# Attention scores as two products of 128 rows and one of 32 rows in two row groups

## The chip, the cores and the metric

The kernel runs on one core of a Trainium2 chip. The metric is the device time of one execution in microseconds (us), the median over runs. Before the change it is 2363.67 us (three runs, 2359.02 to 2363.83).

Engines are named as in the profile: PE is TensorE's matmul, PEld its weight load, DVE is VectorE, ACT ScalarE, POOL GpSimd, and SP is the engine that issues most DMAs. A product on PE has a stationary operand (up to 128 rows by 128 columns, loaded by a LDWEIGHTS on PEld) and a moving operand (the same rows by up to 512 columns). The sum runs over the rows, which are the partitions of on-chip memory where both operands lie. A product whose operands have 32 rows uses one of four 32-row groups of the array.

## The reference, cut to what matters

Two layers, each with latent attention beside a convolution module, and then a gated feed-forward part. What the change touches is the attention's scores: 8 heads, 1024 tokens, 64 "nope" components and 32 rotary ("rope") components a head. The rotary part of the key is one for all heads.

```python
sc = (jnp.einsum("bqhd,bkhd->bhqk", qn, k_nope)
      + jnp.einsum("bqhr,bkr->bhqk", qr, k_rope))
p = jax.nn.softmax(sc.astype(jnp.float32) * scale, axis=-1).astype(v.dtype)
return jnp.einsum("bhqk,bkhd->bqhd", p, v)
```

All is float32. The kernel gets near that accuracy by splitting each operand into a high and a low part, rounded to the one-pass type float32r, and adding three products: high by high, high by low and low by high.

## The kernel before, in words

A layer is three stages. `project` makes the latents, queries, keys and the convolution's input; `attention` makes values, scores, softmax and the weighted sum; `feed` does the output projection and the feed-forward part. PE, DVE, ACT and POOL run in the order in which the program writes them (`manual_schedule`); the DMAs on SP's queue are ordered by a planner, by when their inputs are ready.

Keys and queries are split into high and low parts in `project` and written to scratch in device memory: `kd` (keys, nope), `krd` (key, rope), `qd` (queries, nope) and `qrd` (queries, rope, in two halves of 16 rows). Head 0 (`DIRECT = 1`) doesn't go through scratch: the steps `key`, `query_rope` and `query` also copy its parts from on-chip memory straight into its operand tiles on SP's queue (L566, L567, L592, L607). Every other head is brought in by `load_head` (L249), called in the loop of `attention` when the head before it is at its third block (L1405). A head has four operand tiles (`head_tiles`, L1246): q high, q low, k high, k low, each of 96 rows (64 nope, 32 rope), from a pool with 8 slots ("m"). So a head's tiles come free when the scores of the head two before it are done. Most other large tiles come from a pool of 31 slots ("b", through `blk`).

The attention loop runs over blocks n = head x 8 + query tile, 64 a layer, 128 in all. For one n the order on PE is:

- `turn(n)`: eight transposes (tile t) of the softmax numerators, which ACT copies and DVE subtracts to high and low parts;
- `scores(n + 2)`: six products of 96 rows by 512 columns into a two-bank tile s: for each column half, (high, high), (high, low), (low, high); then DVE takes the negated row maximum mx;
- `expo(n + 1)` on ACT: the exponential of an earlier s;
- `values(...)`: eight products of 128 rows by 256 columns into the tile o.

Beside it, an `agenda` puts other work at given n: the convolution's late taps (`tap_late`, L1438: a product on POOL or ACT, then an addition on POOL or by an accumulating DMA), and from n = 56 on the weights of the output projection (tile wo): POOL issues a DMA of the high half, ACT turns it to its negative (L166, at n = 59), POOL adds the input by DMA (L167).

At the start of a layer's attention PE makes the first value tiles (`rows`, L1271, tile pv) and then the scores of block 0; these need head 0's tiles whole.

Of the kernel before, what the change touches and what calls it, by code (L numbers as in the profile page):

```python
# [10 lines left out]
F32R = mybir.dt.float32r  # L11
# [9 lines left out]
NOPE = 64  # L21
ROPE = 32
HALF = ROPE // 2
# [48 lines left out]
HALVES = (slice(0, 512), slice(512, T))  # L72
# [33 lines left out]
class Encoder:  # L106
# [301 lines left out]
    def project(self, l, carry):  # L408
        nc, a = self.nc, self.a
# [4 lines left out]
        heads = {}  # L414
        qd = [self.dp.tile([HEADS, NOPE, T], F32R, name=f"qd{l}{i}") for i in range(2)]
        qrd = [self.dp.tile([2, HEADS, HALF, T], F32R, name=f"qrd{l}{i}") for i in range(2)]
        kd = [self.dp.tile([HEADS, NOPE, T], F32R, name=f"kd{l}{i}") for i in range(2)]
        krd = [self.dp.tile([ROPE, T], F32R, name=f"krd{l}{i}") for i in range(2)]
        st = {}
# [65 lines left out]
        def latent(name, out, key, j):  # L485
            c = self.blk(f"c{name}{l}")
            nc.vector.tensor_tensor(out=c, in0=ps[name], in1=rx, op=ALU.mult)
            out.append(c)
            if j == 0:
                st[key] = self.blk(f"{key}{l}")  # L490
                nc.scalar.activation(out=st[key], in_=c, func=AF.Square)
                yield 1.22, 0.0
                return
            sq = self.blk(f"{key}{l}_{j}")
            nc.scalar.activation(out=sq, in_=c, func=AF.Square)
            yield 1.22, 1.5
            nc.vector.tensor_tensor(out=st[key], in0=st[key], in1=sq, op=ALU.add)
            yield 1.25, 0.0
# [56 lines left out]
        def key(j):  # L555
            if j == 0:
                heads.update((h, self.head_tiles(l, h)) for h in range(DIRECT))
            p = ps[f"k{j}"]
            kh, kl = self.blk(f"kh{l}_{j}", F32R), self.blk(f"kl{l}_{j}", F32R)
            nc.scalar.copy(out=kh, in_=p)  # L560
            yield 0.0, 1.5
            nc.vector.tensor_tensor(out=kl, in0=p, in1=kh.bitcast(F32), op=ALU.subtract)
            for i, s in enumerate((kh, kl)):
                self.move(kd[i][2 * j:2 * j + 2].rearrange("h d t -> (h d) t"), s)
                for h in range(DIRECT if j == 0 else 0):
                    self.move(heads[h][1][i][0:NOPE, :], s[h * NOPE:(h + 1) * NOPE, :])  # L566
                    self.move(heads[h][1][i][NOPE:96, :], krd[i])  # L567
            yield 1.22, 0.0

        def query_rope(i):  # L570
            p = ps[f"u{i}"]
            c, s = self.blk(f"rc{l}_{i}"), self.blk(f"rs{l}_{i}")
            nc.vector.tensor_tensor(out=c, in0=p, in1=st["cos"], op=ALU.mult)
            nc.vector.tensor_tensor(out=s, in0=p, in1=st["sin"], op=ALU.mult)
            st["rope", i] = c, s
            yield 2.44, 0.0
            if i == 0:
                return
            (c1, s1), (c2, s2) = st.pop(("rope", 0)), st.pop(("rope", 1))
            nc.vector.tensor_tensor(out=c1, in0=c1, in1=s2, op=ALU.subtract)  # L580
            nc.vector.tensor_tensor(out=c2, in0=c2, in1=s1, op=ALU.add)
            his = [self.blk(f"qr{l}_{i}", F32R) for i in range(2)]
            for hi, o in zip(his, (c1, c2)):
                nc.scalar.copy(out=hi, in_=o)
            yield 2.5, 1.0
            for i, (hi, o) in enumerate(zip(his, (c1, c2))):
                nc.vector.tensor_tensor(out=o.bitcast(F32R), in0=o, in1=hi.bitcast(F32), op=ALU.subtract)
                sp = hi, o.bitcast(F32R)
                yield 1.25, 0.0
                for p in range(2):  # L590
                    for h in range(DIRECT):
                        self.move(heads[h][0][p][NOPE + i * HALF:NOPE + (i + 1) * HALF, :],  # L592
                                  sp[p][h * HALF:(h + 1) * HALF, :])
                for p in range(2):
                    self.move(qrd[p][i].rearrange("h d t -> (h d) t"), sp[p], nc.gpsimd)

        def query(j):
            n = self.blk(f"qn{l}_{j}")
            nc.vector.tensor_tensor(out=n, in0=ps[f"n{j}"], in1=st["rq"], op=ALU.mult)
            hi = self.blk(f"qns{l}_{j}", F32R)  # L600
            nc.scalar.copy(out=hi, in_=n)
            yield 1.22, 1.5
            nc.vector.tensor_tensor(out=n.bitcast(F32R), in0=n, in1=hi.bitcast(F32), op=ALU.subtract)
            sp = hi, n.bitcast(F32R)
            for p in range(2):
                for e in range(DIRECT if j == 0 else 0):
                    self.move(heads[e][0][p][0:NOPE, :], sp[p][e * 64:(e + 1) * 64, :])  # L607
                self.move(qd[p][2 * j:2 * j + 2].rearrange("h d t -> (h d) t"), sp[p], nc.gpsimd)
            yield 1.25, 0.0

# [16 lines left out]
        def root(key, out, n, name):  # L627
            st[out] = self.rsqrt_cols(st.pop(key), n, f"{name}{l}", HALVES, self.bank)
            clock["dve"] = max(clock["dve"], clock["pe"] + 1.0) + 3.6
# [21 lines left out]
        for i in range(2):  # L651
            add(f"u{i}", "u2", ranked("u2", i, QL, f"u{i}", cqs), lambda i=i: query_rope(i))
        for j in range(4):
            add(f"n{j}", f"u{j // 2}", ranked(f"u{j // 2}", j % 2, QL, f"n{j}", cqs), lambda j=j: query(j))

        times, starts, t = {}, {}, 0.0
# [14 lines left out]
        hl, rx, ps = self.first_sections(l, supply) if l == 0 else self.next_sections(l, carry, supply)  # L671
# [572 lines left out]
                                            in1=o[:, a:b], op0=ALU.mult, op1=ALU.add)  # L1244

    def head_tiles(self, l, h):  # L1246
        return [[self.tmp("m", f"{n}{l}_{h}{p}", F32R) for p in range(2)] for n in "qk"]

    def load_head(self, l, h, qd, qrd, kd, krd):
        q, k = tiles = self.head_tiles(l, h)  # L1250
        for p in range(2):
            self.move(q[p][0:NOPE, :], qd[p][h])
            for i in range(2):
                self.move(q[p][NOPE + i * HALF:NOPE + (i + 1) * HALF, :], qrd[p][i, h])
            self.move(k[p][0:NOPE, :], kd[p][h])
            self.move(k[p][NOPE:96, :], krd[p])
        return tiles

    def attention(self, l, u, conv, away, spill, kvs, loaded, ahead):
        nc = self.nc  # L1260
        sd = self.dp.tile([HEADS, T], F32, name=f"sd{l}")

        load = lambda h: self.load_head(l, h, *spill)
        state, v = {}, []

        def rows(tt):
# [15 lines left out]
        def scores(n):  # L1282
            h, qt = divmod(n, 8)
            st = state[h]
            q, k = st["qk"]
            qs = slice(qt * 128, (qt + 1) * 128)
            ps = self.wide(f"s{l}_{h}_{qt}")
            for c in range(2):
                cs = slice(c * 512, (c + 1) * 512)
                for s, (i, j) in enumerate(((0, 0), (0, 1), (1, 0))):  # L1290
                    nc.tensor.matmul(ps[:, cs], q[i][0:96, qs], k[j][0:96, cs],  # L1291
                                     start=(s == 0), stop=(s == 2))
            mx = self.cp.tile([128, 1], F32, name=f"mx{l}_{h}_{qt}", tag="mx", bufs=4)
            nc.vector.tensor_reduce(out=mx, in_=ps, op=ALU.max, axis=AX.X, negate=True)  # L1294
            st["s"][qt] = ps, mx
# [98 lines left out]
        for n in range(-2, total + 2):  # L1394
            if 0 <= n < total:
                turn(n)
            for tt in range(4) if n == -2 else (4, 5) if n == -1 else ():
                rows(tt)
            if n + 2 < total:
                h, qt = divmod(n + 2, 8)  # L1400
                if qt == 0:
                    state[h] = {"sums": self.cp.tile([128, 8], F32, name=f"sums{l}_{h}", tag="sums", bufs=3),
                                "s": {}, "p": {}, "pt": {}, "qk": loaded.pop(h)}
                scores(n + 2)
                if qt == 2 and h + 1 < HEADS and h + 1 not in loaded:  # L1405
                    loaded[h + 1] = load(h + 1)
            if 0 <= n + 1 < total:
                expo(n + 1)
            for tt in (6, 7) if n == -1 else ():
                rows(tt)  # L1410
            if n >= 2:
                values(n - 1 - n % 2, n % 2)
            for f in agenda.pop(n, ()):
                f()
# [168 lines left out]
```

## Time and profile before

| what | number |
|---|---|
| median of three runs | 2363.67 us |
| profiled execution, its own time | 2361.39 us |
| span of the profiled execution | 2359.6 us |
| granted clock, mean | 0.996 |
| PE, PEld busy | 2288.0 us (97%), 1919.1 us (81%) |
| DVE, ACT, POOL busy | 1787.7, 1281.3, 825.6 us |
| scores' products (L1291) | 768, 208.0 us busy |
| first and last scores of a layer | layer 0 from 213.6 us; layer 1 to 1589.7 us |

The page gives, for a group of instructions, the line, engine and operation, the tiles written and read, the shape, the count, the busy time in us and the mean of one in ns, and after the second bar the idle time of the engine before them and what ended it. A matmul's record is longer than the distance to the next one, as products run in a pipeline: the distance between starts is what a product costs in a stream. In a timeline a row is a run of equal instructions: start, length, engine, line, operation, tiles, shape, count, and in brackets the idle time before it.

### The profile page before, as it was taken

Reading aid. Unit: us, or ns where it says so; the run is one execution under the profiler, and the core shown is the slowest. Engines: PE = TensorE matmul, PEld = TensorE weight load, DVE = VectorE, ACT = ScalarE, POOL = GpSimd, SP = SyncE. Lnnn points to the kernel's source line nnn. Section 1 sums busy time; section 2 is a strip of 40 time slices with the busy share of each in tenths; the row PEclk is TensorE's granted clock in tenths of the full one; section 3 lists DMA queues with packets and bytes.
Section 4 is the critical chain, followed back from the end, with each engine's and each line's share of the span. In section 5 each row is a group of like instructions: output and inputs, shape, how many; then the busy total and the mean of one; then the engine's idle time right before and its main releaser. Section 6 shows DMA issues by size and latency. Waiting matters only on the chain.

```text
span 2359.6 us, 31729 instructions
## 1 busy us (share of the span) xinstructions
PE 2288.0 (97%) x11138; PEld 1919.1 (81%) x11138; DVE 1787.7 (76%) x2412; ACT 1281.3 (54%) x2040; POOL 825.6 (35%) x840
## 2 busy tenths in 40 slices
PE   8999999998999999999999999999989999999997
PEld 6887899786788888888888888987867888888885
DVE  5988888768777777776559778886787777768664
ACT  4444877535655555544523468774465555555442
POOL 2222798512333232001413248963222333320032
PEclk9999999999999999999999999999999999999998
DMA  5888964935899998935968988547459999988365
GB/s 178 154 178 267 205 134 98 243 105 128 214 284 279 274 274 218 314 123 143 208 132 167 223 231 185 120 98 219 134 134 253 272 281 278 273 207 308 100 137 143
DMA packets 193168, 467.03 MB, mean 198 GB/s; under 512 B 26608, under 2 KB 32624, under 8 KB 193008
## 3 DMA queue, kind: packets, MB, share of 16 engines
q0 software_dynamic: 104288, 225.73, 46.0%
q1 hardware_dynamic: 88720, 239.27, 30.9%
q8 instruction: 88, 1.44, 0.3%
q14 instruction: 72, 0.59, 0.1%
HBM read 309.81 MB, written 80.41 MB: 165 GB/s over the span
## 4 chain that ended last, share of the span: by engine, by line
PE 82%; DVE 5%; issue 5%; ACT 3%; DMA 3%; POOL 2%; POOLq 0%; SPq 0%; ACTq 0%; DVEq 0%
PE p L915 31%; PE pd L1106 14%; PE po L766 7%; PE s L1291 6%; PE o L1344 4%; PE t L1318 4%; PE pa L202 3%; PE pq L202 2%; PE pkv L202 2%; PE pg L202 2%; PE pn L202 1%; PE pg L405 1%; PE pv L1271 1%; PE pu L202 1%; PE pa L405 1%
## 5 line engine op out<-in xcount | busy, mean ns | idle before, releaser
L915 PE MATMUL p<-b,w 128*128 128x512 f32 x3552 | 814.2, 391 | 23.7 <-DVE zv L864 7.5
L915 PEld LDWEIGHTS p<-b,w 128*128 128x128 f32 x3552 | 667.5, 188 | 169.7 <-DVE zv L864 9.2
L1106 PE MATMUL pd<-ab,wd 128*128 128x512 f32 x1848 | 420.7, 390 | 0.2 <-DMA wd<-in_w_down 0.2
L1106 PEld LDWEIGHTS pd<-ab,wd 128*128 128x128 f32 x1848 | 346.6, 188 | 72.4 <-DMA wd<-in_w_down 0.6
L1321 DVE TENSOR_TENSOR pt<-t,pt 128x512 fp32r<-128x512 f32 x256 | 164.6, 685 | 64.9 <-ACT pt L1320 64.9
L1291 PE MATMUL s<-k,q 96*128 96x512 f32 x768 | 208.0, 406 | 0.0
L167 POOL DMA_DIRECT2D w<-wu x92 | 79.2, 861 | 323.6 <-ACT w L166 292.6
L1320 ACT CAST pt<-t 128x512 fp32r<-128x512 f32 x256 | 137.5, 590 | 52.5 <-PE t L1318 46.0
L167 POOL DMA_DIRECT2D w<-in_w_up x116 | 101.7, 888 | 181.4 <-ACT w L166 177.5
L1442 POOL TENSOR_TENSOR late<-gate,par 128x1012 f32<-128x1012 f32 (+12 forms) x78 | 159.7, 2048 | 0.0
L1294 DVE TENSOR_REDUCE mx<-s 128x1 f32<-128x1024 f32 x128 | 155.8, 1217 | 0.0
L1291 PEld LDWEIGHTS s<-k,q 96*128 96x128 f32 x768 | 135.2, 189 | 22.6
L864 DVE TENSOR_TENSOR zg<-p,zg 128x512 f32<-128x512 f32 x88 | 60.6, 690 | 115.7 <-PE p L915 70.1
L1344 PEld LDWEIGHTS o<-pt,v 128*128 128x128 f32 x1024 | 139.6, 191 | 9.9
L1302 ACT ACTIVATE p<-s,mx 128x1024 f32<-128x1024 f32 x128 | 145.1, 1133 | 0.0
L1429 DVE SCALAR_TENSOR_TENSOR conv<-gate,par,conv 128x1009 f32<-128x1009 f32 (+7 forms) x112 | 142.3, 1274 | 3.6 <-ACT conv L467 1.0
L1318 PE MATMUL t<-ident,p 128*128 128x128 f32 x1024 | 133.5, 273 | 10.9 <-ACT p L1302 10.9
L1344 PE MATMUL o<-pt,v 128*128 128x256 f32 x1024 | 143.6, 284 | 0.0
L711 POOL DMA_DIRECT2D wd<-in_w_down x44 | 32.7, 748 | 308.0 <-PE pd L1106 305.7
L1229 ACT CAST ab<-ac 128x512 fp32r<-128x512 f32 x130 | 80.2, 617 | 101.5 <-DVE ac L1042 98.8
L166 ACT ACTIVATE w<-w 128x512 fp32r<-128x512 f32 x208 | 130.7, 629 | 2.9
L1318 PEld LDWEIGHTS t<-ident,p 128*128 128x128 f32 x1024 | 114.3, 141 | 15.7 <-ACT p L1302 15.2
(1975 smaller groups left out, 4244.7 us busy)
## 6 DMA issues: line engine op xcount, KB each, us to landing
w<-in_w_up POOLq DMA_DIRECT2D x232, 256.0 KB, 7.4
wu<-in_w_up SPq DMA_DIRECT2D x88, 512.0 KB, 4.8
w<-wu POOLq DMA_DIRECT2D x92, 256.0 KB, 4.6
sd<-in_w_down SPq DMA_DIRECT2D x44, 512.0 KB, 10.0
ws<-sd SPq DMA_DIRECT2D x44, 512.0 KB, 3.8
wd<-in_w_down POOLq DMA_DIRECT2D x88, 256.0 KB, 5.4
act<-v SPq DMA_DIRECT2D x36, 512.0 KB, 5.6
ac<-act SPq DMA_DIRECT2D x72, 256.0 KB, 6.1
```

The costliest lines, as they stand in the source:

```text
L167: self.nc.gpsimd.dma_start(out=lo, in_=src, accum_op=ALU.add)
L202: nc.tensor.matmul(ps[:, HALVES[c]], w, x[:, HALVES[c]], start=(k == 0 and s == 0), stop=(k == n - 1 and s == 2))
L766: nc.tensor.matmul(ps[c, m], p[:, sl], q[:, HALVES[c]], start=(k == 0 and t == 0), stop=(k == 3 and t == 2))
L915: nc.tensor.matmul(ps, w[p][:, k * 128:(k + 1) * 128], b[:, q], start=(i in (1, 5, 2) and k == 0 and t == 0), stop=(k == 3 and t == 2), sk ...
L1106: nc.tensor.matmul(ps[t, m], w[i, j][p][:, m * 128:(m + 1) * 128], b[:, q], start=(i in (1, 5, 2) and j == 0 and s == 0), stop=(j == half ...
L1291: nc.tensor.matmul(ps[:, cs], q[i][0:96, qs], k[j][0:96, cs], start=(s == 0), stop=(s == 2))
L1294: nc.vector.tensor_reduce(out=mx, in_=ps, op=ALU.max, axis=AX.X, negate=True)
L1302: nc.scalar.activation(out=p, in_=ps, func=AF.Exp, bias=mx, accum_out=st["sums"][:, qt:qt + 1])
L1318: nc.tensor.transpose(tp[:, i, :], p[:, kt * 128:(kt + 1) * 128], self.ident)
L1321: nc.vector.tensor_tensor(out=pt[1][g][:, :, qi * 128:(qi + 1) * 128], in0=tp, in1=hi.bitcast(F32), op=ALU.subtract)
L1344: nc.tensor.matmul(po, v[kt][:, h // 2, e, :], pt[s][kt // 4][:, kt % 4, :], start=(kt == 0 and s == 0), stop=(kt == 7 and s == 1))
L1442: self.nc.gpsimd.tensor_tensor(out=p[:, lo:hi], in0=u[:, lo + s:hi + s], in1=self.tap(l, j, t).broadcast_to([128, hi - lo]), op=ALU.mult)
```

## The change

Per head there are now five tiles. With h and l for the high and low parts:

| tile | rows 0 to 63 | rows 64 to 95 | rows 96 to 127 |
|---|---|---|---|
| q1 | q nope h | q nope l | (l goes on) |
| k1 | k nope l | k nope h | (h goes on) |
| q2 | q nope h | q rope h | q rope h |
| k2 | k nope h | k rope h | k rope l |
| q3 | q rope l in rows 0 to 31 and again in 32 to 63 | | |

k3 holds k rope h in rows 0 to 31 and again in 32 to 63. It is loaded once a layer, at the start of `attention`. The products q1 k1 and q2 k2 have 128 rows and are made for both column halves, four products. The last part, q rope l by k rope h, has 32 rows: the left column half uses rows 0 to 31 of q3 and k3 (row group 0), the right half rows 32 to 63 (row group 1). The sum is the same three products as before. q1, q2, k1 and k2 take the four "m" slots of a head; q3 and k3 come from "b". What is held twice is copied twice: the loads of a head are 16 DMAs in place of 10.

```diff
     def head_tiles(self, l, h):
-        return [[self.tmp("m", f"{n}{l}_{h}{p}", F32R) for p in range(2)] for n in "qk"]
+        t = {n: self.tmp("m", f"{n}{l}_{h}", F32R) for n in ("q1", "q2", "k1", "k2")}
+        t["q3"] = self.blk(f"q3{l}_{h}", F32R)
+        return t
+
+    def put_key(self, t, p, src):
+        if p == 0:
+            self.move(t["k2"][0:NOPE, :], src)
+            self.move(t["k1"][NOPE:128, :], src)
+        else:
+            self.move(t["k1"][0:NOPE, :], src)
+
+    def put_key_rope(self, t, p, src):
+        self.move(t["k2"][NOPE + p * ROPE:NOPE + (p + 1) * ROPE, :], src)
+
+    def put_query(self, t, p, src):
+        if p == 0:
+            self.move(t["q2"][0:NOPE, :], src)
+            self.move(t["q1"][0:NOPE, :], src)
+        else:
+            self.move(t["q1"][NOPE:128, :], src)
+
+    def put_query_rope(self, t, p, i, src):
+        for r in range(2):
+            lo = (p == 0) * NOPE + r * ROPE + i * HALF
+            self.move(t["q3" if p else "q2"][lo:lo + HALF, :], src)
 
     def load_head(self, l, h, qd, qrd, kd, krd):
-        q, k = tiles = self.head_tiles(l, h)
+        t = self.head_tiles(l, h)
         for p in range(2):
-            self.move(q[p][0:NOPE, :], qd[p][h])
+            self.put_query(t, p, qd[p][h])
+            self.put_key(t, p, kd[p][h])
+        for p in range(2):
             for i in range(2):
-                self.move(q[p][NOPE + i * HALF:NOPE + (i + 1) * HALF, :], qrd[p][i, h])
-            self.move(k[p][0:NOPE, :], kd[p][h])
-            self.move(k[p][NOPE:96, :], krd[p])
-        return tiles
+                self.put_query_rope(t, p, i, qrd[p][i, h])
+            self.put_key_rope(t, p, krd[p])
+        return t
...
         load = lambda h: self.load_head(l, h, *spill)
+        k3 = self.blk(f"k3{l}", F32R)
+        for r in range(2):
+            self.move(k3[r * ROPE:(r + 1) * ROPE, :], spill[3][0])
...
-            for c in range(2):
-                cs = slice(c * 512, (c + 1) * 512)
-                for s, (i, j) in enumerate(((0, 0), (0, 1), (1, 0))):
-                    nc.tensor.matmul(ps[:, cs], q[i][0:96, qs], k[j][0:96, cs],
-                                     start=(s == 0), stop=(s == 2))
+            for i in (1, 2):
+                for cs in HALVES:
+                    nc.tensor.matmul(ps[:, cs], t[f"q{i}"][:, qs], t[f"k{i}"][:, cs], start=(i == 1), stop=False)
+            for c, cs in enumerate(HALVES):
+                rows = slice(c * ROPE, (c + 1) * ROPE)
+                nc.tensor.matmul(ps[:, cs], t["q3"][rows, qs], k3[rows, cs], start=False, stop=True)
```

In `key`, `query_rope` and `query` the direct copies of head 0 call the same helpers in place of their own `move`.

More of the change, by code (lines that the diff above doesn't have):

```diff
@@ L565, in key @@
                 for h in range(DIRECT if j == 0 else 0):
-                    self.move(heads[h][1][i][0:NOPE, :], s[h * NOPE:(h + 1) * NOPE, :])
-                    self.move(heads[h][1][i][NOPE:96, :], krd[i])
+                    self.put_key(heads[h], i, s[h * NOPE:(h + 1) * NOPE, :])
+                    self.put_key_rope(heads[h], i, krd[i])
             yield 1.22, 0.0
@@ L591, in query_rope @@
                     for h in range(DIRECT):
-                        self.move(heads[h][0][p][NOPE + i * HALF:NOPE + (i + 1) * HALF, :],
-                                  sp[p][h * HALF:(h + 1) * HALF, :])
+                        self.put_query_rope(heads[h], p, i, sp[p][h * HALF:(h + 1) * HALF, :])
                 for p in range(2):
@@ L606, in query @@
                 for e in range(DIRECT if j == 0 else 0):
-                    self.move(heads[e][0][p][0:NOPE, :], sp[p][e * 64:(e + 1) * 64, :])
+                    self.put_query(heads[e], p, sp[p][e * 64:(e + 1) * 64, :])
                 self.move(qd[p][2 * j:2 * j + 2].rearrange("h d t -> (h d) t"), sp[p], nc.gpsimd)
@@ L1284, in scores @@
             st = state[h]
-            q, k = st["qk"]
+            t = st["qk"]
             qs = slice(qt * 128, (qt + 1) * 128)
             ps = self.wide(f"s{l}_{h}_{qt}")
-            for c in range(2):
-                cs = slice(c * 512, (c + 1) * 512)
-                for s, (i, j) in enumerate(((0, 0), (0, 1), (1, 0))):
-                    nc.tensor.matmul(ps[:, cs], q[i][0:96, qs], k[j][0:96, cs],
-                                     start=(s == 0), stop=(s == 2))
+            for i in (1, 2):
[4 more added lines that the diff above has]
+                nc.tensor.matmul(ps[:, cs], t["q3"][rows, qs], k3[rows, cs], start=False, stop=True)
             mx = self.cp.tile([128, 1], F32, name=f"mx{l}_{h}_{qt}", tag="mx", bufs=4)
```

## The prediction

> **What bounds the kernel now.** I read the page first (busy time, groups), then the windows of the attention stage, then the timeline of single blocks of it.
>
> ```profile
> span 2359.6 us, 31729 instructions
> PE 2288.0 (97%) x11138; PEld 1919.1 (81%) x11138; DVE 1787.7 (76%) x2412; ACT 1281.3 (54%) x2040; POOL 825.6 (35%) x840
> ...
> L1106 PE MATMUL pd<-ab,wd 128*128 128x512 f32 x1848 | 420.7, 390 | 0.2 <-DMA wd<-in_w_down 0.2
> ...
> L1291 PE MATMUL s<-k,q 96*128 96x512 f32 x768 | 208.0, 406 | 0.0
> ...
> L1318 PE MATMUL t<-ident,p 128*128 128x128 f32 x1024 | 133.5, 273 | 10.9 <-ACT p L1302 10.9
> L1344 PE MATMUL o<-pt,v 128*128 128x256 f32 x1024 | 143.6, 284 | 0.0
> ```
>
> TensorE is busy for 97% of the span. A stream of 512-column products moves at 420.7/1848 = 228 ns a product, while one record lasts 390 ns, so 162 ns of it lie under the next one. The scores are 768 of them, six to a block, 128 blocks in all. The next fence holds windows of layer 0 (columns: time, then busy time of PE, PEld, DVE, ACT, POOL with instruction counts, clock, DMA share, GB/s).
>
> ```profile
> 230.00:300.00 70.00, 68.10 (x464) 61.93 (x463) 56.31 (x76) 57.15 (x102) 55.69 (x39) 1.00 0.96 202
> 300.00:390.00 90.00, 90.00 (x620) 82.94 (x619) 76.73 (x102) 67.56 (x128) 86.08 (x47) 1.00 0.56 121
> ```
>
> In the steady part PE has no gap at all (90.00 of 90.00), the clock is whole, and the DMA engines are full only up to about 300 us (0.96). One block of the timeline:
>
> ```profile
> 301.80 1.03 PE L1318 MATMUL t<-ident,p 128*128 128x128 f32 x8
> 302.59 1.62 PE L1291 MATMUL s<-k,q 96*128 96x512 f32 x6
> 304.05 1.12 PE L1344 MATMUL o<-pt,v 128*128 128x256 f32 x8
> 305.01 1.04 PE L1318 MATMUL t<-ident,p 128*128 128x128 f32 x8
> 305.80 0.94 PE L1291 MATMUL s<-k,q 96*128 96x512 f32 x3
> ```
>
> A block takes 305.80 - 302.59 = 3.21 us: eight transposes at (1.03 - 0.273)/7 = 108 ns, eight value products at (1.12 - 0.284)/7 = 119 ns, which is 1.82, and 1.39 for the six scores, 231 each. So a nanosecond taken from or added to the scores is a nanosecond of the block, wherever PE is the bound. It is not the bound everywhere: the answer on the score tile counts who waited for what follows from it.
>
> ```profile
>   PE t L1318: 10.9, 16
> ```
>
> In 16 of 128 blocks the transposes waited for the exponential on ACT. That leaves 112 blocks in which a change of PE time counts.
>
> **The change, part by part.**
>
> *The products.* Four of 128 rows take the place of four of six with 96. Their pitch stays: 96-row ones have 231, 128-row ones 228. The last two are of 32 rows and stand in row groups 0 and 1. Removed: two 96-row products, 2 x 228 = 456 ns. Added: the pair. Three prices make it: how long after the first the second starts, and what the array loses at the change from 128-row to 32-row products and back.
>
> ```profile
> 303.14 0.19 PEld L1291 LDWEIGHTS s<-k,q 96*128 96x128 f32 x1
> ...
> 303.14 0.39 PE L1291 MATMUL s<-k,q 96*128 96x512 f32 x1
> ```
>
> The load of the next product starts when the running product starts (303.14 both), one ahead, and a load with its short product follows the last at 108 ns (the transposes). If that order holds in the pair, the second load starts with the first product of the pair and the second product 108 ns behind it: the pair takes 108 + 228 = 336, and a block gains 120. The bounds of this price: 0 (both loads done beforehand, the pair takes 228) and 228 (one behind the other). I take 108, since the loads in the rows run one ahead and no more.
>
> *The change of row tile.* No product before has under 96 rows, so no row shows it. Lower bound 0: going from 96-row to 128-row products in each block costs nothing beyond the pitches above. Upper bound, as long as loads run ahead: the 162 ns by which one record lies under the next are exposed. It is paid twice a block. Between far ends neither row is nearer, so I take half, 80. Per block that is -120 + 2 x 80 = +40 ns, between -120 and +204; over 112 blocks **+4.5 us**, between -13.4 and +22.8. The Trainium skill ("TensorEngine Tiling (Array Packing)", Key Properties) says that changing the tiling mode, and not just the tile, drains the engine. It gives no time for it, and no run here shows it yet; by it the zero end falls away, and what is saved by overlap may be paid out again at the two changes.
>
> *The first head's operands.* Head 0 goes from SBUF straight into its tiles on SP's queue, just ahead of the first scores.
>
> ```profile
> 195.21 1.62 SPq L114 DMA_DIRECT2D q<-qr  x2
> 197.52 1.61 SPq L114 DMA_DIRECT2D q<-rc  x2
> 199.25 2.01 SPq L114 DMA_DIRECT2D q<-qns  x1
> 201.37 1.85 SPq L114 DMA_DIRECT2D q<-qn  x1
> ...
> 213.41 1.34 PEld L1291 LDWEIGHTS s<-k,q 96*128 96x128 f32 x6
> ```
>
> The answer on DMAs for 195 to 203 us (KB each, median us to landing):
>
> ```profile
> DMA packets 311, 1.02 MB, mean 128 GB/s; under 512 B 65, under 2 KB 65, under 8 KB 310
> ...
> q<-qns SPq DMA_DIRECT2D x1, 256.0 KB, 11.5
> q<-qn SPq DMA_DIRECT2D x1, 256.0 KB, 11.5
> q<-qr SPq DMA_DIRECT2D x2, 64.0 KB
> ```
>
> The last piece lands at 201.37 + 11.5 = 212.9, half a us before the scores' first weight load at 213.41. This cover is thin. The change adds ahead of that point a second copy of the high nope part (256 KB), four more 16-row rope copies (4 x 64) and both halves of k3 (2 x 128): 768 KB. The two big pieces land 2.1 us apart, 256 KB in 2.1 us, so the upper bound is 6.3 - 0.5 = 5.8 us of PE wait per layer. Lower bound 0: before 203 us the engines move a mean of 128 GB/s only, and k3's source exists long before, so these extras may slip in early. The value products' rows, the DVE maxima and ACT all stand behind this wait, and little of it is made up. I take 4 a layer, nearer the upper bound, as only the small copies have early sources on hand: **+8 us**. Nothing reads the spilled keys at that time, so the one more issue in the key step costs nothing.
>
> *Loads of heads 1 to 7.* From ten DMAs (1.5 MB) to sixteen: six of 256 KB, eight of 64, two of 128, 2.3 MB. Head 2's load in the busy part:
>
> ```profile
> q<-qd SPq DMA_DIRECT2D x2, 256.0 KB, 10.5
> k<-kd SPq DMA_DIRECT2D x2, 256.0 KB, 10.3
> ...
> q<-qrd SPq DMA_DIRECT2D x4, 64.0 KB, 8.4
> k<-krd SPq DMA_DIRECT2D x2, 128.0 KB, 10.0
> ```
>
> ```profile
> 239.92 0.45 SPq L114 DMA_DIRECT2D q<-qd  x1
> ...
> 250.58 1.30 SPq L114 DMA_DIRECT2D k<-krd  x1
> ```
>
> They were issued from 239.9 to 250.6 and took 8 to 10 us to land, some 20 us together. They may start when the tiles of two heads earlier are free and have eight blocks, 8 x 3.21 = 25.7 us. Half as much again is about 26 to 30 if the queue is the limit: at the edge for heads 1 to 3, covered later (DMA share 0.56). I take 1 us a layer (0 to 4): **+2**. If the load came late, PE would stand at the head's first score. The one more block tile per head and k3 need room among 31 slots; I put that at 0: four inputs and four outputs of the convolution, eight value tiles, four of y and rb and six of ys make 26 at most. If room fails, late taps on POOL wait, not PE.
>
> *Sum.* 4.5 + 8 + 2 = 14.5 on the profiled execution's 2361.4, so 2375.9. The median of the runs, 2363.7, is 2.3 above that execution, so I predict **2378** (0.6% slower). The range of this case alone runs from -13.4 + 0 to 22.8 + 11.6 + 8, 2350 to 2406.
>
> **The rivals.**
>
> *A, the pair fully side by side, no price at the changes (not slower).* For it: loads have time beside the product ahead (190 of 228 ns); against it: they run one ahead in every row. A block then saves 228, 112 blocks 25.5. Part is given back by work that keeps its own pace:
>
> ```profile
> 410.07 2.22 POOL L711 DMA_DIRECT2D wo<-in_w_o  x4
> 419.59 3.50 POOL L167 DMA_DIRECT2D wo<-in_w_o  x4 [7.31 <-ACT wo L166]
> ```
>
> ```profile
> 418.66 2.19 ACT L166 ACTIVATE wo<-wo 128x512 fp32r<-128x512 f32 x4
> ```
>
> POOL is busy 86 of 90 us with the late taps, so it issues the first output weights at 410.1 to 412.3 whatever PE does, and ACT turns them at 418.66, where block 59 stands in its order, ahead of an exponential. ACT can get there at most 418.7 - 412.3 = 6.4 us earlier, and PE with it, where A would want 12.7 in this layer: 6 lost. A: -25.5 + 6 + 10 = -9.5, 2354. The point from which it decides: the sum turns to faster when a block saves more than 10/112 = 90 ns. The Trainium skill ("TensorE: Matmul & The Clock Gate", Part 3) has products in different row groups start about 4 ns apart, with 3.07 times the speed from four tiles; by that it is this case, apart from the changes of mode.
>
> *B, the array must be empty before the next weights are loaded.* Then the loads lose their cover too.
>
> ```profile
> 208.04 0.50 PE L1271 MATMUL pv<-wv0h,kvs_0h 128*128 128x512 f32 x1 [1.32 <-DVE qn L599]
> 208.38 0.40 PE L1271 MATMUL pv<-wv0l,kvs_0h 128*128 128x512 f32 x1
> ```
>
> A first product after a wait lasts 0.10 longer: its load in the open. From the fourth product to the first value product: 390 + 100 + 108 + 390 + 100 = 1088 in place of 3 x 228 = 684, +404 a block, +45 us; with the 10 of the loads 2361.4 + 55 + 2.3 = 2419. For it: all hangs on one unknown change; against: loads run ahead everywhere now.
>
> *C, no overlap at all.* The 32-row products queue as any two do: 2 x 80 a block for the changes, +18 us, with the loads 2392 (2374 with free changes). For it: nothing in the rows shows two products at once.
>
> **How the numbers follow.** Chances: the forecast 0.46 (0.12 of it faster, 0.07 the same, 0.27 slower), A 0.20 (0.18 faster, 0.02 same), B 0.20 and C 0.14 (0.13 slower, 0.01 same). The bound is 0.2%, 4.7 us, about what a measurement of this kernel tells from no change. Faster 0.30, same 0.10, slower 0.60. The range for 8 in 10 goes from below A's sum with a free start of the head (2347) to near B's (2416).
>
> **What would show it.** Right: 112 blocks at about 3.25 us in the attention timeline, pairs starting some 110 ns apart, a gap of under 0.16 us at each change of row tile, and PE idle ahead of each layer's first scores for about 4 us with a DMA into q or k3 as its end. A would show blocks of 2.98 and ACT waiting for output weights; B blocks of 3.6 and weight loads that start only after a product's end; C the second of the pair 228 ns behind the first. My forecast is wrong if the blocks are under 3.1 us, or if the first scores start on time.

## The result and the profile after

The changed kernel takes 2404.37 us (median of 4 runs, 2401.16 to 2405.81). The kernel before, run beside it, takes 2362.26. The ratio is 1.0178, 95% interval 1.0161 to 1.0196: slower by 42 us, where 14.5 were forecast. The profiled execution of the changed kernel took 2403.27 us.

The page after, in its lines on span and busy time:

```profile
span 2401.5 us, 31889 instructions
PE 2315.8 (96%) x11138; PEld 1888.8 (79%) x11138; DVE 1787.1 (74%) x2412; ACT 1282.8 (53%) x2040; POOL 825.5 (34%) x840
```

TensorE issues the same 11138 products as before and is busy 27.8 us longer (2288.0 before); the other 14 us are idle time. The waits of PE, longest first (us in total, times, longest):

```profile
PE s L1317 <- DMA q<-qn: 17.3, 2, 9.4
PE t L1346 <- ACT p L1330: 9.6, 16, 1.4
```

The first row is new: the first scores of each of the two layers wait for the first head's query. The second row answers to the 10.9 us on the exponential before, in the same 16 blocks.

**Where the time went.** One stretch of a layer runs from its first transpose to its first output product. These rows are the two ends in layer 0, first in the timeline before, then after:

```profile
221.91 0.27 PE L1318 MATMUL t<-ident,p 128*128 128x128 f32 x1
...
433.14 0.48 PE L766 MATMUL po<-ys_1h,wo 128*128 128x512 f32 x1
```

```profile
235.20 0.27 PE L1346 MATMUL t<-ident,p 128*128 128x128 f32 x1
...
455.19 0.48 PE L765 MATMUL po<-ys_1h,wo 128*128 128x512 f32 x1
```

The stretch grew from 211.23 to 219.98 us, 8.75 us, and in layer 1 by 8.75 as well. In layer 0 it began 13.29 us late. From the first value product of a layer to this first transpose it is 25.4 us in place of 13.9 in layer 0, and 26.2 in place of 13.8 in layer 1: 11.5 and 12.3 longer. So 17.5 us went into the blocks and 23.8 into the two starts. Another 1.8 lies ahead of the first value product of layer 0. It isn't put down to the change, as kernels with the same instructions up to there have that product at 207.8 to 209.8 us (before: 208.0). About 1.2 was given back elsewhere, and the span is 41.9 longer.

**A block.** The timeline after, around 340 us (start, duration): PE, then the last 128-row product of this block by itself, then PEld.

```profile
338.30 1.04 PE L1346 MATMUL t<-ident,p 128*128 128x128 f32 x8
339.09 1.17 PE L1317 MATMUL s<-k,q 128*128 128x512 f32 x4
340.18 0.50 PE L1320 MATMUL s<-k,q 32*128 32x512 f32 x2
340.61 1.22 PE L1372 MATMUL o<-pt,v 128*128 128x256 f32 x8
341.67 1.03 PE L1346 MATMUL t<-ident,p 128*128 128x128 f32 x8
```

```profile
339.86 0.40 PE L1317 MATMUL s<-k,q 128*128 128x512 f32 x1
```

```profile
339.63 0.19 PEld L1317 LDWEIGHTS s<-k,q 128*128 128x128 f32 x1
340.18 0.18 PEld L1320 LDWEIGHTS s<-k,q 32*128 32x128 f32 x2 [0.36 <-issue]
...
340.61 0.41 PEld L1372 LDWEIGHTS o<-pt,v 128*128 128x128 f32 x3 [0.24 <-DVE pt L1349]
```

The block takes 341.67 - 338.30 = 3.37 us (3.21 before). The two 32-row loads fit into one span of 0.18 us and the two products into one of 0.50: in the single records the products start 3 ns apart. So the pair is fully side by side. But the weight loads no longer run ahead at a change of row tile, from products of 128 rows to products of 32 or back. PEld stands still for 0.36 us, the pair's loads start with its products at 340.18, and the loads of the value products start with them at 340.61. The last 128-row product starts at 339.86; its successor in an unbroken stream would have come 228 ns later, and the pair comes after 327 (single records), so the array stood for 99 ns, which I read as a drain. The load of the pair then lies in the open: its records are some 107 ns longer than others. Going back costs about 90 and 107 again. From the last 128-row product to the second value product it is 979 ns, where 228 + 228 + 119 = 575 would stand without changes: **404 ns for two changes, 0.2 us each.** The 979 ns are 971 to 983 in all 118 blocks in which the value products follow the pair; how the 404 divide into drain and load is a reading of the records. Against that stand 1386 - 5 x 228 = 246 ns saved by the shorter stream, which leaves +158 ns a block. The Trainium skill ("TensorEngine Tiling (Array Packing)", Key Properties) says that a change of tiling mode drains the engine; the trace agrees with 99 and about 90 ns; the load in the open, about as long again, comes on top.

**The start of a layer.** PE around the first scores of layer 0, then windows of the same place and of layer 1 (columns as before: time, busy time of PE, PEld, DVE, ACT, POOL, clock, DMA share, GB/s):

```profile
223.42 1.19 PE L1317 MATMUL s<-k,q 128*128 128x512 f32 x2 [7.85 <-DMA q<-qn]
...
227.57 0.63 PE L1298 MATMUL pv<-wv0h,kvs_1h 128*128 128x512 f32 x1
228.00 0.63 PE L1298 MATMUL pv<-wv0l,kvs_1h 128*128 128x512 f32 x1
```

```profile
215.40:223.40 8.00, 0.17 (x1) 0.01 (x1) 3.14 (x9) 0.65 (x2) 0.00 (x0) 0.79 1.01 313
223.40:230.20 6.80, 6.78 (x16) 4.65 (x17) 1.66 (x3) 0.65 (x2) 0.00 (x0) 0.50 1.03 320
...
1409.50:1416.50 7.00, 6.91 (x19) 4.83 (x20) 1.96 (x3) 0.65 (x2) 0.00 (x0) 0.63 0.90 284
```

The kernel before, from its first score to its first transpose in layer 0:

```profile
213.60:222.00 8.40, 8.40 (x38) 6.73 (x37) 7.21 (x16) 4.96 (x11) 0.53 (x1) 1.00 1.02 395
```

PE waits 7.85 us and 9.40 us, and then it runs at half clock: products 427 ns apart (227.57 to 228.00) and a clock of 0.50 until 230.2. From the first score to the first transpose it is 11.8 and 11.0 us instead of 8.3, 3.5 and 2.7 more. About 0.3 of this are the changes of row tile in the two blocks of scores that stand there (experiment 5, which has no wait, takes 8.57), so the clock costs 3.2 and 2.4. The Trainium skill ("TensorE: Matmul & The Clock Gate", Part 1) has the clock halved after an idle window of about 3.4 us until a busy one has passed; the trace agrees with 0.50 and 0.63 behind these waits, and with 1.00 in the same place before. The half clock lasted about 6.8 us behind the first wait and 5 behind the second (0.63 over 7.00 us), longer than one such window.

Why the query is late shows in the SP queue and in the DMA answer for 204 to 214 us (packets, MB, share of 16 engines; then KB each and median us from issue to landing):

```profile
196.97 1.44 SPq L114 DMA_DIRECT2D q<-qr  x2
199.24 1.14 SPq L114 DMA_DIRECT2D q<-rc  x2
200.49 3.27 SPq L114 DMA_DIRECT2D q<-qr  x2
204.26 3.50 SPq L114 DMA_DIRECT2D q<-rc  x2
207.87 3.76 SPq L114 DMA_DIRECT2D q<-qns  x2
211.72 2.25 SPq L114 DMA_DIRECT2D q<-qn  x1
```

```profile
q0 software_dynamic: 905, 3.28, 88.3%
q1 hardware_dynamic: 161, 0.35, 13.1%
...
qd<-qns POOLq DMA_DIRECT2D x3, 512.0 KB, 20.7
q<-qns SPq DMA_DIRECT2D x2, 256.0 KB, 10.2
```

The same two queues before, 202 to 212 us, between the issue of the last piece and its landing:

```profile
q0 software_dynamic: 724, 2.61, 72.2%
q1 hardware_dynamic: 218, 0.65, 28.9%
```

Four additional rope copies (64 KB each) stand ahead of the big pieces of the query. Their issue lasts from 200.49 to 207.87, and it falls into the time in which POOL's stores of the other heads' queries fill the engines: these moved 3.28 MB in the 10 us and SP's queue 0.35, about half of the 0.65 that it had before while it waited for its last piece. So the first big piece is issued at 207.87 in place of 199.25, and the last, behind one more copy of 256 KB, at 211.72 in place of 201.37 (1.8 of this the queue was late at its start). From the last issue to the first score it is 11.7 us, as long as that piece took to land before (11.5): the query is late because it is issued late. The Trainium skill ("DMA: Bandwidth & Descriptors", Queues, rings and completion order) has each engine go round the queues that it has work for, packet by packet. The trace shows both queues served, but 905 packets against 161, and 724 against 218 before, so the shares were far from equal here. Whether SP's queue had work waiting at every engine all that time, no view shows.

### The profile page after: what moved, and what is told of

Same layout as the page of the kernel before. It is cut to its first block, busy times and chain, and to the rows that moved or that the text cites. A ratio compares the mean times of both kernels' runs of the same rounds, so it can differ in the third digit from the quotient of the medians.

```text
span 2401.5 us, 31889 instructions
## 1 busy us (share of the span) xinstructions
PE 2315.8 (96%) x11138; PEld 1888.8 (79%) x11138; DVE 1787.1 (74%) x2412; ACT 1282.8 (53%) x2040; POOL 825.5 (34%) x840
## 4 chain that ended last, share of the span: by engine, by line
PE 76%; issue 7%; DMA 5%; DVE 5%; ACT 3%; POOL 2%; SPq 0%; POOLq 0%; ACTq 0%; DVEq 0%
PE p L914 30%; PE pd L1105 14%; PE o L1372 5%; PE s L1317 4%; PE t L1346 4%; PE po L765 4%; PE pa L202 3%; PE s L1320 2%; PE pq L202 2%; PE pkv L202 2%; PE pg L202 2%; PE pn L202 1%; PE pg L405 1%; DMA q<-qn 1%; DMA wo<-in_w_o 1%
## 5 line engine op out<-in xcount | busy, mean ns | idle before, releaser
L1317 PE MATMUL s<-k,q 128*128 128x512 f32 x512 | 151.1, 417 | 17.3 <-DMA q<-qn 17.3
L1372 PE MATMUL o<-pt,v 128*128 128x256 f32 x1024 | 155.0, 295 | 0.0
L1372 PEld LDWEIGHTS o<-pt,v 128*128 128x128 f32 x1024 | 129.4, 189 | 29.1 <-issue 17.1
L1228 ACT CAST w<-wu 128x512 fp32r<-128x512 f32 x88 | 54.2, 620 | 133.4 <-DVE wu L863 129.3
```

The lines of the kernel that those rows point to most:

```text
L1317: nc.tensor.matmul(ps[:, cs], t[f"q{i}"][:, qs], t[f"k{i}"][:, cs], start=(i == 1), stop=False)
L1372: nc.tensor.matmul(po, v[kt][:, h // 2, e, :], pt[s][kt // 4][:, kt % 4, :], start=(kt == 0 and s == 0), stop=(kt == 7 and s == 1))
```

## The experiments

All times are medians beside runs of the kernel before on the same chip (2362.6 to 2364.6 us); ratios are to that kernel, with their 95% interval. "The stretch" is the one from first transpose to first output product, in layer 0 (before: 211.2 us, after: 220.0).

**1. The third product by 128 rows again.**

```diff
-nc.tensor.matmul(ps[:, cs], t["q3"][rows, qs], k3[rows, cs], start=False, stop=True)
+nc.tensor.matmul(ps[:, cs], t["q1"][:, qs], t["k1"][:, cs], start=False, stop=True)
```

> The changed kernel, but the last two products of a block have 128 rows: they take the first pair of operands once more in place of the 32-row ones, so the scores lack the low rope part and hold the first product twice; all loads stay. Theory S (each change of row tile costs about 0.2 us, as the weight load loses its cover and the array runs empty; the 32-row pair itself costs one product): the block falls from 3.37 to 3.21 us, 112 blocks give 18 us back, 2404 becomes 2386, and the 24 us left are the starts of the two layers, with a wait of 8 to 9 us ahead of each first score. Rival L (the longer block comes from the fuller operands or the larger loads): the block stays near 3.37 and the time near 2404.

Measured: 2381.6 us, 1.0067 [1.005, 1.0084]. The stretch is 211.29 us, the blocks 3.22. Two rows of its timeline, the last two products of successive blocks, 3.23 us apart:

```profile
344.25 0.62 PE L1320 MATMUL s<-k,q 128*128 128x512 f32 x2
...
347.48 0.62 PE L1320 MATMUL s<-k,q 128*128 128x512 f32 x2
```

All operands are loaded as in the changed kernel, and six products of 128 rows take what six of 96 took. So the whole loss in the blocks comes with the 32-row pair. The waits at the starts stay (8.1 and 8.2 us), and the kernel stays 17 us above the one before.

**2. Both 32-row products in one row group.**

```diff
-rows = slice(c * ROPE, (c + 1) * ROPE)
+rows = slice(0, ROPE)
```

> The changed kernel, but both 32-row products use rows 0 to 31, one row group. Theory S: the second now queues behind the first, 0.22 us more a block, 3.60 us, over 108 to 112 blocks 24 us more, 2428. Rival N (the two starts 3 ns apart in the records are an artefact and the pair never ran side by side): block and time as in the changed kernel, 3.37 and 2404.

Measured: 2430.6 us, 1.0277 [1.0256, 1.0297], blocks 3.61, the stretch 232.95. The pairs of two successive blocks:

```profile
340.42 0.73 PE L1320 MATMUL s<-k,q 32*128 32x512 f32 x2
...
344.02 0.73 PE L1320 MATMUL s<-k,q 32*128 32x512 f32 x2
```

A block lost 0.24 us more, one product's pitch (its distance to the next). The second copies do what they are for: they make the pair cost one product.

**3. All value rows ahead of the first scores.**

```diff
-for tt in range(4) if n == -2 else (4, 5) if n == -1 else ():
+for tt in range(8) if n == -2 else ():
     rows(tt)
...
-for tt in (6, 7) if n == -1 else ():
-    rows(tt)
```

> The changed kernel, but all eight value tiles of a layer are made ahead of the first scores, in place of four: 5.5 us more of PE work in front of the wait. Theory D (the first head's operands land some 8 us late, and the long idle halves the clock for the next 7 us, which costs 3 more): the wait falls to 2 to 4 us, the clock stays whole, the softmax starts about 1.3 us later than its scores allow; per layer 5.5 + 3 - 1.3 = 7 us less, 2404 becomes 2390. Rival W (the wait moves along, as the value tiles' work delays the same loads): 2400 or more, with a wait still over 6 us.

Measured: 2393.11 us, 1.0118 [1.01, 1.0135]. The first scores of layer 0 in its timeline:

```profile
222.12 1.15 PE L1317 MATMUL s<-k,q 128*128 128x512 f32 x4 [1.36 <-DMA q<-qn]
```

The loads land about as late as in the changed kernel (222.1 against 223.4), but PE has other work until then. The kernel is 28.5 us above the one before in place of 42: 13.6 us come back. The blocks stay at 3.37.

**4. The 32-row products apart, so that a block has four changes.**

```diff
 for i in (1, 2):
     for cs in HALVES: ...  # two 128-row products
-for c, cs in enumerate(HALVES): ...  # the pair
+    c, cs = i - 1, HALVES[i - 1]
+    ...  # one 32-row product of the pair
```

> The changed kernel, but the two 32-row products of a block stand apart, one after the first two 128-row products and one at the end: four changes of row tile a block in place of two, and nothing left to run side by side. Theory S: two more changes at 0.2 and one more product of 0.23, 0.63 us more a block, 4.0 us, over 112 blocks 70 us more, 2474. Rival O (one price a block, however often the tile changes): 0.23 more, 3.60, and 2429.

Measured: 2476.09 us, 1.0469 [1.0448, 1.049], blocks 4.00. The transposes of two successive blocks:

```profile
346.69 1.04 PE L1347 MATMUL t<-ident,p 128*128 128x128 f32 x8
...
350.69 1.03 PE L1347 MATMUL t<-ident,p 128*128 128x128 f32 x8
```

That is 0.63 us a block more than the changed kernel: 0.23 for the pair that no longer runs side by side, and 0.40 for two more changes. The price of 0.2 us a change, read from single records above, is here a difference of whole blocks.

**5. The stores for the other heads behind the first head's loads.** They are collected in a list and issued by SP after the loads of k3, instead of by POOL at once.

```diff
...
-self.move(qd[p][2 * j:2 * j + 2].rearrange("h d t -> (h d) t"), sp[p], nc.gpsimd)
+self.stores.append((qd[p][2 * j:2 * j + 2].rearrange("h d t -> (h d) t"), sp[p]))
...
     self.move(k3[r * ROPE:(r + 1) * ROPE, :], spill[3][0])
+for dst, sp in self.stores:
+    self.move(dst, sp)
```

> The same work as the changed kernel, but the query stores for heads 1 to 7 (4.5 MB a layer, issued by POOL) are issued by SP after the first head's loads and the two of k3. Theory P (the first head's loads crawl because they share full DMA engines with these stores: 20 to 50 KB a us on SP's queue against 340 on POOL's): the idle ahead of the first scores falls from 7.9 and 9.4 us to under 3 in each layer, the half clock after it goes, 2380 to 2390. Rival V (what counts is the larger number of copies that SP issues, whatever else moves): the idle stays, 2400 or more. What could be late next: head 1's loads behind the stores, seen as idle PE about 27 us after the first scores.

Measured: 2376.51 us, 1.0058 [1.004, 1.0076]: 28 us off the changed kernel. PE at the first scores of layer 0, and the landing of the same loads, 197 to 207 us:

```profile
213.26 0.39 PE L1302 MATMUL pv<-wv0h,kvs_1l 128*128 128x512 f32 x1
213.49 1.07 PE L1321 MATMUL s<-k,q 128*128 128x512 f32 x4
```

```profile
q<-qns SPq DMA_DIRECT2D x2, 256.0 KB, 3.2
q<-qn SPq DMA_DIRECT2D x1, 256.0 KB, 4.8
```

The first and the last issue of the head's query in SP's queue:

```profile
195.07 1.46 SPq L114 DMA_DIRECT2D q<-qr  x2
...
204.56 0.74 SPq L114 DMA_DIRECT2D q<-qn  x1
```

All the added bytes and copies are still there, and the waits are gone: the last piece is issued 9.5 us behind the first copy in place of 14.8, it lands in 4.8 us in place of 11.7, there is no gap, and the clock stays whole. The stores are twelve of 512 KB a layer, 6 MB and not the 4.5 that were expected. Before the change the same stores ran beside fewer copies, and PE didn't wait either. So neither the added copies nor the stores make the wait alone: it takes both on the engines at one time. What remains is the blocks: the stretch is 220.03 us, and 221.0 in layer 1.

**6. Edits 1, 3 and 5 together.**

> Three edits together: the third product by 128 rows again (q1 and k1 once more; leaves out the low rope part and holds the first product twice), all value rows ahead of the first scores, and the stores behind the first head's loads. If the changes of row tile and the start of a layer are all that the change costs, this is back at the kernel before: blocks 3.22 us, 2360 to 2368. If something else costs too (more bytes, later heads' loads, room in SBUF), it stays above 2372.

Measured: 2365.56 us, 1.0013 [1.0001, 1.0024], blocks 3.22. With the changes of row tile and the late start both gone, the kernel is back within 0.13% of the one before (0.24% at most by the interval, under 6 us). So the additional bytes, block tiles and later heads' loads cost little, unless edits 3 and 5 save elsewhere what these cost; that was not separated.

**7. Row groups of 64 instead of 32.**

```diff
-rows = slice(c * ROPE, (c + 1) * ROPE)
-nc.tensor.matmul(ps[:, cs], t["q3"][rows, qs], k3[rows, cs], start=False, stop=True)
+rows = slice(c * NOPE, (c + 1) * NOPE)
+nc.tensor.matmul(ps[:, cs], t["q1"][rows, qs], t["k1"][rows, cs], start=False, stop=True)
```

> As the changed kernel, but the pair has 64 rows each: the upper and lower half of q1 and k1 in two row groups of 64 (leaves out the low rope part and adds half products of the first again). Theory S (the price is that of a change of tile size, in and out, whatever the size): blocks 3.37 us and 2400 to 2408. Rival R (only 32-row tiles cost it): blocks about 3.0 us, 2355 to 2370.

Measured: 2404.27 us, 1.0173 [1.0157, 1.0189], the same as the changed kernel. PE and PEld of one block:

```profile
341.00 1.17 PE L1317 MATMUL s<-k,q 128*128 128x512 f32 x4
342.10 0.50 PE L1320 MATMUL s<-k,q 64*128 64x512 f32 x2
342.53 1.22 PE L1372 MATMUL o<-pt,v 128*128 128x256 f32 x8
```

```profile
342.10 0.18 PEld L1320 LDWEIGHTS s<-k,q 64*128 64x128 f32 x2 [0.36 <-issue]
```

The same gap of 0.36 us and the same pitch to the value products (0.43): the price is one of changing the tile size, and not of 32 rows.

**8 to 11. One change for two blocks.** If a change costs 0.2 us, paying it half as often should turn the sign. Four copies of q3 and k3 in four row groups let the 32-row products of two blocks stand together; for the odd block they come first and its 128-row products add to them.

```diff
+def small(n):  # even blocks only
+    ...
+    st["odd"] = self.wide(f"s{l}_{h}_{qt + 1}")
+    for e, ps in enumerate((st["s"][qt][0], st["odd"])):
+        qs = slice((qt + e) * 128, (qt + e + 1) * 128)
+        for c, cs in enumerate(HALVES):
+            rows = slice((2 * e + c) * ROPE, (2 * e + c + 1) * ROPE)
+            nc.tensor.matmul(ps[:, cs], st["qk"]["q3"][rows, qs], k3[rows, cs], start=(e == 1), stop=(e == 0))
+    ...
```

In the first of these kernels this part stands halfway through the even block's value products, with edits 3 and 5.

> The whole computation. The 32-row products of two blocks stand together in four row groups (four copies of q3 and k3), halfway through the value products of the even block, so that an array change into 32 rows and out again is paid once for two blocks; value rows first and stores behind the loads as in the run with three edits. Theory S (0.2 us for each change, products in different row groups side by side): two blocks take 8 x 228 + 228 + 411 = 2463 ns of scores in place of 12 x 231 = 2772 before, 155 ns a block less, 112 blocks -17 us, of which about 6 are given back to work that keeps its own pace, and up to 5 for the start: 2348 to 2358, below the kernel before (2363). Rival Q (four groups don't run side by side, or the odd block's tile, which is claimed a block earlier, or the later maximum holds PE): blocks of 3.2 us or more, 2366 or more.

Measured: 2412.85 us, 1.0204 [1.0186, 1.0221]. The four do not run together:

```profile
346.53 0.18 PEld L1336 LDWEIGHTS s<-k,q 32*128 32x128 f32 x2
...
347.08 0.19 PEld L1336 LDWEIGHTS s<-k,q 32*128 32x128 f32 x2 [0.37 <-ACT p L1352]
```

The second pair waits for the exponential that still reads the tile which the odd block now claims a block earlier, and a steady head takes 27.6 us (27.1 in the changed kernel). Head 1's first scores also wait for its keys, 14.1 us in the two layers. So the four groups are moved behind all value products:

> As the kernel with four row groups, but the four 32-row products stand behind all value products of the even block (119 x 4 = 0.48 us later), where the exponential that frees the odd block's tile is nearly done. Theory S: the wait for that exponential shrinks from 0.55 us to 0.2 or less, all four start within 10 ns where it is gone, two blocks take 6.1 to 6.3 us (before: 6.42): 2354 to 2368. Rival Q (the maximum and the exponential of the even block, now later, hold the next transposes; PE loses there what it wins here): two blocks take 6.5 us or more, 2372 or more.

Measured: 2384.84 us, 1.0085 [1.0067, 1.0104]. The pairs now start 80 ns apart in most of the blocks, and two blocks take 6.34 us, 0.09 less than before the change. A head takes 25.5 us in place of 25.8. But head 1's first scores wait:

```profile
PE s L1321 <- DMA k<-krd: 15.6, 2, 11.1
```

Head 1's loads stand behind the stores on SP's queue, and there are four more copies for a head; in experiment 5, without these four, that wait was 0.7 us. Loading k3 earlier was tried on top:

> As the run before it, with k3 loaded in the key step, some 30 us ahead of the first scores, instead of behind the first head's loads. If those four copies are what holds the first 32-row products of a layer (14.1 us of waits behind k3 in two layers, partly beside other work), 3 to 6 us less than that run; if the room that k3 takes earlier makes another tile late, no gain or a loss.

Measured: 2380.52 us, 1.0062 [1.0038, 1.0085]; the difference to the run before it, 4.3 us, is not clear of the spread of the two (2378 to 2387 and 2373 to 2385). Then head 1's loads ahead of the other heads' stores, with the old order of the value rows:

```diff
-for dst, sp in self.stores:
+for dst, sp in self.stores[:6]:
+    self.move(dst, sp)
+loaded[1] = load(1)
+for dst, sp in self.stores[6:]:
     self.move(dst, sp)
```

> The four row groups behind the value products, k3 loaded in the key step, value rows in their old order, and on SP's queue: the stores that hold head 1, then head 1's loads, then the other stores. In the two runs before, pairs of blocks took 6.34 us in place of 6.43 (a head 25.5 in place of 25.8), but the pair ahead of head 1's first scores took 13.2 and 19.3 us (11.3 and 16.5 with k3 early), as its operands came late, and the start of a layer cost 3.1 and 1.6 us more than in the kernel before. If that is all that kept them above the kernel before, both go: 7 x 0.3 us a layer less than before, 2357 to 2364. If a later load or a tile's room takes the place of head 1's, it stays above 2368.

Measured: 2381.74 us, 1.0077 [1.0061, 1.0092]. Its waits of PE:

```profile
PE t L1371 <- ACT p L1355: 15.9, 6, 6.2
PE s L1325 <- DMA k<-krd: 7.4, 3, 3.6
```

The steady heads are again at 25.5 us, and the wait moved: 15.9 us on exponentials, 12.2 of it in one wait in the first head of each layer, and 7.4 on later heads' keys. The two long waits fall in the time in which the later stores still hold their tiles; that this is their cause was not tested. No version was found that beats the kernel before; what four groups can win in the steady part is 0.3 us a head, about 4 us in all.

## Why the prediction was right or wrong

The direction, slower, was right, and 2404 lies inside the range of 2347 to 2416. The forecast of 2378 was 26 us short. By its steps:

- **The products.** Right: four products of 128 rows at a pitch near 228 ns, and a block of 3.22 us when all six are of 128 rows (experiment 1).
- **The pair.** Priced too dear: I let the second product start 108 ns behind the first, by the order of loads in the transposes. They start 3 ns apart, so the pair costs 228 ns and not 336. Rival A had this right (though not its free changes), and rival C's pair, 228 ns apart, is ruled out; experiment 2 prices running side by side at 0.24 us a block. This error hid part of the next one.
- **The change of row tile.** This step failed. I halved a bound of 162 ns that held only "as long as loads run ahead", and they do not: a change costs 0.2 us, not 0.08, which the records divide into a drain of 90 to 99 ns and a load of 107 ns in the open. Rival B had the loads right and the size too high: its block was 3.6, for it added a full drain of 162 ns and a pair one load apart. Experiments 4 (0.40 us for two more changes) and 7 (64 rows cost the same) settle it. The block came out at +0.16 us instead of +0.04, 17.5 us instead of 4.5.
- **The first head's operands.** This step failed too, with 23.8 us against 8. Two things were missing. The price of 2.1 us for 256 KB came from the end of the loads before, where SP's queue had 29% of the engines. The added rope copies were issued into POOL's stores, which left that queue 13%: four copies of 64 KB held it for 7.4 us, where that price gives 2.1, and the waits were 7.9 and 9.4 us. My upper bound of 5.8 was no bound, since it counted the added bytes and left out the queue beside them. It fell short although it counted too many bytes: k3's 256 KB are issued at 214.06, behind the query. And behind the wait the clock was half, which cost 3.2 and 2.4 us more. Experiment 5 removes all of it by moving the stores alone.
- **Loads of heads 1 to 7.** Forecast +2, measured about 0: in the changed kernel no later head waits for a load. Only when the stores were moved did head 1's loads become late.
- **Room in the slots.** Forecast 0; experiment 6 is within 0.13% of the kernel before with the same tiles.

## What to carry to other kernels

Products of fewer rows in several row groups did run side by side here, but going into another tile size and back cost about 0.4 us in total, nearly two products of 512 columns; they pay only when what stands between two changes saves more than that. A transfer ahead of a first use is not priced by its bytes alone: look at which queue fills the engines at that time, put what is needed first ahead of it in one queue, and then look at what stands behind it. The long waits of PE here, of 7.5 us and more, cost more than their length, because the clock was half for 4 to 10 us afterwards.

## What the runs showed of the hardware that was not expected

- A change of tile size costs 0.2 us, the same for 64 and 32 rows. The records divide it into 90 to 99 ns of drain and a weight load of 107 ns that nothing covers, about the same in both directions.
- Two products in two row groups, each with its own load, start 3 ns apart, loads 4 ns apart, and take the pitch of one.
- After 7.5 us or more of idle PE, the clock was half until 4.0 to 9.7 us behind the wait in all ten such waits (the two starts of the changed kernel and of experiments 1, 2, 4 and 7). After waits of 2 to 3 us this came only in some cases: of two waits of 2.84 us in the kernel before, it came behind the one that ended at 588 us and not behind the one at 1753.
- While two queues compete for the DMA engines, the shares can be very unequal: 3.28 MB for POOL's stores and 0.35 MB for SP's loads in the same 10 us.
